# Convolution steps and bank copies re-ordered at the block boundaries of a decoder layer's up projection, and one weight sum moved from a DMA to VectorE

## The chip, the core and the metric

The kernel runs on one core of a Trainium2 chip. The metric is the device time of one execution in microseconds (us). TensorE does the matmuls, ScalarE (ACT in the profile) and VectorE (DVE) the elementwise work, GpSimd (POOL) and SyncE (SP) mostly issue DMAs.

## What is computed

The reference is one layer of a decoder for 512 prompt tokens and 8 sample tokens (520 columns), width 2048, in float32. The part that the change touches is the ConvFFN:

```python
h = rmsnorm(x, lw['ffn_norm_w']) @ lw['w_up']              # 2048 -> 2 * 5632
hp = jnp.concatenate([conv_buf, h], axis=1)
hc = cw[0] * hp[:, 0:L] + cw[1] * hp[:, 1:L + 1] + cw[2] * hp[:, 2:L + 2] + lw['conv_b']
hg, hu = jnp.split(hc, 2, axis=-1)
x = x + (jax.nn.silu(hg) * hu) @ lw['w_down']
```

Around it stand an input projection with attention and a gated spatial mix before, and a per-layer embedding gate after.

## The kernel before

**Layout and matmuls.** Activations lie transposed: 128 features on the partitions, 520 tokens in two halves of 260 columns. Every float32 matmul is made of three, since each operand is split into a part `hi` that is rounded to float32r and a rest `lo`: hi·hi, hi·lo, lo·hi.

**The weight stream.** All weights come as blocks of eight 128x128 tiles (512 KB, 128x1024 elements) in one fixed order. At the start of block v (`block_start`, L252) the program issues the loads that the table `acts` names for this block, and splits block v+2: ScalarE casts it to `hi` (L249), VectorE subtracts for `lo` (L250). There are three buffers each for `hi` and `lo`, so the cast for v+2 waits until TensorE is through with block v-1. In effect each engine gets its work for a boundary when TensorE passes that boundary, and TensorE has two more blocks before it needs the result.

**The up projection** (`ffn_up`, L1275; `wpair`, L341) works on 44 pairs: gate tile j and up tile 44+j together. Each pair is done by a Winograd-like 2x2 scheme with seven products in place of eight. A product is one block: 8 weight tiles, 3 matmuls each, 24 matmuls of 260 columns (L381). The products run in the order P5, P1, P2, P6, P4, P7, P3 and gather in four PSUM banks: P5 and P3 in bank b, P1, P6 and P7 in bank a, P2 in c, P4 in d. Between two products in one bank, ScalarE copies the bank to SBUF (`snap`, L351: `sn` after P5 and P1, `un` after P6 and P7); the next product in that bank must wait for this copy. So P6 must not begin before `sn` has been copied from bank a after P1, one block (P2) later. VectorE forms the two results `c1` (gate) and `c2` (up) from banks and copies (L355, L360, L362, L366).

**The sums of weights.** The seven products need weight sums. `winograd` (L108) puts into `acts` a load of r21 into a buffer S and three DMAs that add to S in place (r22, r11, r12), a load of r11 into a buffer L and one DMA that adds r21 to it, and plain loads of r12 and r22 (buffers `st`). The adding DMAs are issued by GpSimd (L261). S + r11 is needed by the cast for P6, S + r12 by the cast for P3, L + r21 by the cast for P7.

**The convolution.** `conv_half` (L1244) and `conv_pair` (L1261) are generators. For `c2` after P7 and for `c1` after P3: VectorE multiplies by the norm's factor R into `hb` (L1250, L1251), ScalarE makes the last tap (L1252) and two small state copies (L1253, L1254), VectorE the other two taps (L1256, L1258), then ScalarE the Silu (L1265), VectorE the product with the other half (L1268, L1271), and SyncE stores it to `fd` (L1273). One `next` is made per boundary, so that VectorE's step and the ScalarE step that reads it stand at the same boundary. Within a boundary the order is: loads, cast and rest of block v+2, GpSimd's sums, convolution steps, and last the bank copies and combinations (`late`).

**The end of the stage.** In the last pair, `f_parts` (L1306) already loads back the first eleven `fd` tiles and splits them (L430 is its VectorE part). After it `flush` (L269) runs what is left of the convolution at once, and the down projection begins.

Of the kernel before, what the change touches and what calls it, by code (L numbers as in the profile page):

```python
# [171 lines left out]
class Kernel:  # L172
    def __init__(self, ctx, tc, a):
# [63 lines left out]
    def load_block(self, b):  # L237
        self.nc.sync.dma_start(self.wtmp("st", b), self.a["w"][b])

    def split_block(self, v, part=(0, BLK)):  # L240
        if v >= NV:
            return
        t = self.st[WS.src[v]]
# [4 lines left out]
        hi, lo = self.hi[v], self.lo[v]  # L248
        self.nc.scalar.copy(hi[:, c], t[:, c])  # L249
        self.nc.vector.tensor_sub(lo[:, c], t[:, c], hi[:, c].bitcast(F32))  # L250

    def block_start(self, v):  # L252
        if v > 0:
            acts = WS.acts[v]
            for what, kind, r, src in acts:
                if what == "load":
                    self.nc.sync.dma_start(self.wtmp(kind, r), self.a["w"][src])
            self.split_block(v + 2)
            for what, kind, r, src in acts:
                if what == "sum":  # L260
                    self.nc.gpsimd.dma_start(self.st[kind, r], self.a["w"][src], accum_op=ALU.add)  # L261
        for g in list(self.conv):
            if next(g, None) is None:
                self.conv.remove(g)
        for f in self.late.pop(v, ()):
            f()
        self.tick()

    def flush(self):  # L269
        for f in self.late.pop(self.pos // BLK, ()):  # L270
            f()
        for g in self.conv:
            for _ in g:
                pass
        self.conv = []

    def at_block(self, ahead, f):
        self.late[self.pos // BLK + ahead].append(f)

    def tick(self):  # L280
        for g in list(self.bg):
# [56 lines left out]
            if k == nk - 1:  # L338
                done(n, ps[n])

    def wpair(self, name, n1, n2, X, done1, done2):  # L341


        nc = self.nc
        bank, c = {}, {}
        part = lambda t, h: t[:, h * HW:(h + 1) * HW]

        def snap(z, key, h):
            if key not in c:
# [1 line left out]
            nc.scalar.copy(part(c[key], h), bank[z][:, 0:HW])  # L351

        def after_p2():
            c["c1"] = self.slot(name="c1")
            nc.vector.tensor_add(part(c["c1"], 0), bank["c"][:, 0:HW], part(c["sn"], 0))  # L355

        def after_p7():
            c["c2"] = self.slot(name="c2")
            snap("a", "un", 1)
            nc.vector.scalar_tensor_tensor(out=part(c["c2"], 1), in0=bank["a"][:, 0:HW], scalar=-1.0, in1=part(c["sn"], 1),  # L360
                                           op0=ALU.mult, op1=ALU.subtract)
            nc.vector.tensor_sub(part(c["c2"], 0), bank["d"][:, 0:HW], part(c["un"], 1))  # L362
            done2(c["c2"])

        def after_p3():
            nc.vector.tensor_add(part(c["c1"], 1), bank["b"][:, 0:HW], part(c["un"], 0))  # L366
            done1(c["c1"])

        after = {"P5": lambda: snap("b", "sn", 1), "P1": lambda: snap("a", "sn", 0), "P2": after_p2, "P6": lambda: snap("a", "un", 0),
                 "P7": after_p7, "P3": after_p3}  # L370
        for p in PRODUCTS:
            z = BANK[p]
            new = z not in bank
            if new:
                bank[z] = self.aux("w" + z)
            ps = bank[z][:, 0:HW]
            for i in range(len(X[p])):
                whi, wlo = self.wtile((name, p, n1, i))
                xh, xl = X[p][i][:, 0:HW], X[p][i][:, HW:NT]
                for q, (w, x) in enumerate(((whi, xh), (whi, xl), (wlo, xh))):  # L380
                    nc.tensor.matmul(ps, lhsT=w, rhs=x, start=new and i == 0 and q == 0, stop=i == len(X[p]) - 1 and q == 2,  # L381
                                     skip_group_check=True)
# [853 lines left out]
    def conv_input(self, n):

        hb = self.slot(name="hb")
        self.nc.gpsimd.memset(hb[:, 0:2], 0.0)
        sv = hb[:, 2 + S:2 + S + 3 * NS].rearrange("p (b r) -> p b r", b=NS)  # L1240
        self.nc.gpsimd.tensor_copy(sv[:, :, 0:2], self.sc[:, n, :].rearrange("p (b r) -> p b r", b=NS))
        return hb

    def conv_half(self, hb, t, n):  # L1244
# [3 lines left out]
        sv = hb[:, 2 + S:2 + S + 3 * NS].rearrange("p (b r) -> p b r", b=NS)
        R, tv = self.v2(self.R), self.v2(t)
        nc.vector.tensor_mul(hb[:, 2:2 + S].rearrange("p (h w) -> p h w", h=2), tv[:, :, 0:HP], R[:, :, 0:HP])  # L1250
        nc.vector.tensor_mul(sv[:, :, 2].rearrange("p (h w) -> p h w", h=2), tv[:, :, HP:HW], R[:, :, HP:HW])  # L1251
        nc.scalar.activation(t[:, 0:m], hb[:, 2:2 + m], AF.Identity, scale=self.col("cw2", n), bias=self.col("cb", n))  # L1252
        nc.scalar.copy(self.cst[:, n, 0:2], hb[:, S:S + 2])  # L1253
        nc.scalar.copy(self.cst[:, n, 2:2 + NS], sv[:, :, 2])  # L1254
        yield True
        nc.vector.scalar_tensor_tensor(out=t[:, 0:m], in0=hb[:, 1:1 + m], scalar=self.col("cw1", n), in1=t[:, 0:m],  # L1256
                                       op0=ALU.mult, op1=ALU.add)
        nc.vector.scalar_tensor_tensor(out=t[:, 0:m], in0=hb[:, 0:m], scalar=self.col("cw0", n), in1=t[:, 0:m],  # L1258
                                       op0=ALU.mult, op1=ALU.add)

    def conv_pair(self, j, hg, tg, tu):  # L1261
        nc = self.nc
        m = S + 3 * NS
        yield from self.conv_half(hg, tg, j)
        nc.scalar.activation(tg[:, 0:m], tg[:, 0:m], AF.Silu)  # L1265
        yield True
        fv = self.v2(hg)
        nc.vector.tensor_mul(fv[:, :, 0:HP], tg[:, 0:S].rearrange("p (h w) -> p h w", h=2),  # L1268
                             tu[:, 0:S].rearrange("p (h w) -> p h w", h=2))
        sm = lambda z: z[:, S + 2:S + 2 + 3 * NS].rearrange("p (h w r) -> p h w r", h=2, r=3)[:, :, :, 0]  # L1270
        nc.vector.tensor_mul(fv[:, :, HP:HW], sm(tg), sm(tu))  # L1271
        yield True
        nc.sync.dma_start(self.fd[j], hg[:, 0:NT])  # L1273

    def ffn_up(self):  # L1275
        nc, a = self.nc, self.a
# [6 lines left out]
        def begin(g):  # L1283
            self.drain(self.gr)
            next(g)
            self.conv.append(g)

        for j in range(KF):
            if j == KF - 1:
                self.finish_fine()  # L1290
# [1 line left out]
            hg, hu = self.conv_input(j), self.conv_input(KF + j)
            up = []

            def done2(t, j=j, hu=hu, up=up):
                up.append(t)
                begin(self.conv_half(hu, t, KF + j))

            def done1(t, j=j, hg=hg, up=up):
                begin(self.conv_pair(j, hg, t, up[0]))  # L1300

            self.wpair("up", j, KF + j, self.X, done1, done2)
# [232 lines left out]
```

## Time and profile before

| | us |
|---|---|
| runs of the kernel: 3090.12, 3087.09, 3089.05; median | 3089.05 |
| the profiled execution's own time | 3091.61 |
| its span, first to last instruction | 3089.9 |
| up projection, from its first matmul (L381) to the end of its last, in the span | 1157.4 to 2368.8 |
| TensorE busy, whole span | 2836.5 |
| mean granted TensorE clock | 0.947 |

The profile is of one execution. A group's row gives the line, engine, operation and operands, the count, the busy time and the mean of one, then the engine's idle time just before these instructions and what ended it. A row of stretches gives busy time and instruction count per engine, then the granted TensorE clock (1.00 is full), the DMA engines' busy share and GB/s. A row of the timeline gives the start, the duration, the engine and the instruction, and in brackets an idle time before it with its releaser. SPq and POOLq are DMA issues; the time to landing runs from the issue to the completion.

### The profile page before, as it was taken

To read this page: it belongs to the slowest core of one execution; us is meant where nothing else is said; L and a number is where in the kernel's file an instruction comes from. 1 tells how busy PE (TensorE), PEld (TensorE's weight loads), DVE (VectorE), ACT (ScalarE), POOL (GpSimd) and SP (SyncE) were. 2 spreads that over 40 slices of the span, in tenths; PEclk is the share of its full clock that TensorE was granted. 3 is DMA by queue.
4 is the path that set the end of the run, shared out by engine and by line. 5 is a ranking of instruction groups with operands and counts; after the bars stand their busy time and mean duration, and the time that the engine had idled before them with its cause. 6 is when DMAs were issued, how large, how long until landed. Compare 5 with 4: busy or idle time off the path is not lost.

```text
span 3089.9 us, 53347 instructions
## 1 busy us (share of the span) xinstructions
PE 2836.5 (92%) x22836; PEld 2824.4 (91%) x22836; DVE 1528.7 (49%) x2265; ACT 1093.2 (35%) x1775; POOL 219.7 (7%) x425
## 2 busy tenths in 40 slices
PE   9999999999999987888888888888888999999999
PEld 9999999999999987887777887777888999999999
DVE  5666454533334356555555555555556333324543
ACT  5465432222223344334333334334334222232321
POOL 0101000000000001111111111111110000000000
PEclk9999999999999998888888888888888999999999
DMA  5223232323323455666666676666676433332232
GB/s 172 96 76 125 69 102 89 92 83 96 96 89 121 144 156 140 164 171 162 163 161 164 167 171 165 156 165 164 168 170 183 151 125 113 117 102 90 85 125 86
DMA packets 124429, 404.08 MB, mean 131 GB/s; under 512 B 14160, under 2 KB 15312, under 8 KB 124192
## 3 DMA queue, kind: packets, MB, share of 16 engines
q1 hardware_dynamic: 97344, 303.49, 30.0%
q0 software_dynamic: 26848, 97.18, 17.0%
q8 instruction: 179, 2.93, 0.4%
q14 instruction: 58, 0.48, 0.0%
HBM read 375.49 MB, written 25.12 MB: 130 GB/s over the span
## 4 chain that ended last, share of the span: by engine, by line
PE 74%; DVE 11%; ACT 8%; issue 6%; DMA 0%; SPq 0%; ACTq 0%; POOL 0%; DVEq 0%
PE mm L318 19%; PE mm L322 19%; PE mm L320 19%; PE wa L381 11%; ACT hi L249 6%; PE wd L381 4%; DVE lo L250 4%; DVE c L1258 2%; DVE c L1256 2%; ACT sn L351 1%; DVE c L366 0%; ACT cst L1253 0%; DVE hb L1251 0%; PE po L916 0%; DVE c L362 0%
## 5 line engine op out<-in xcount | busy, mean ns | idle before, releaser
L250 DVE TENSOR_TENSOR lo<-st,hi 128x1024 fp32r<-128x1024 f32 (+1 forms) x398 | 485.3, 1220 | 723.5 <-ACT hi L249 719.4
L381 PE MATMUL wa<-X,hi 128*128 128x260 f32 x2112 | 466.4, 322 | 229.9 <-ACT sn L351 229.9
L249 ACT CAST hi<-st 128x1024 fp32r<-128x1024 f32 (+1 forms) x398 | 414.3, 1041 | 684.3 <-PE mm L320 439.1
L381 PEld LDWEIGHTS wa<-X,hi 128*128 128x128 f32 x2112 | 390.1, 226 | 239.4 <-ACT sn L351 239.4
L318 PE MATMUL mm<-xnh,hi 128*128 128x260 f32 x1920 | 394.6, 288 | 5.5 <-ACT hi L249 5.5
L320 PE MATMUL mm<-xnl,hi 128*128 128x260 f32 x1920 | 386.9, 282 | 0.3 <-DVE xnl L433 0.3
L322 PE MATMUL mm<-xnh,lo 128*128 128x260 f32 x1920 | 386.9, 283 | 0.0
L381 PE MATMUL wa<-X,lo 128*128 128x260 f32 x1056 | 331.4, 314 | 0.0
L318 PEld LDWEIGHTS mm<-xnh,hi 128*128 128x128 f32 x1920 | 296.1, 189 | 5.6 <-ACT hi L249 5.5
L320 PEld LDWEIGHTS mm<-xnl,hi 128*128 128x128 f32 x1920 | 300.1, 191 | 0.6 <-DVE xnl L433 0.6
L250 DVE TENSOR_TENSOR lo<-S,hi 128x1024 fp32r<-128x1024 f32 x132 | 161.8, 1226 | 272.7 <-ACT hi L249 272.7
L322 PEld LDWEIGHTS mm<-xnh,lo 128*128 128x128 f32 x1920 | 294.0, 189 | 0.0
L318 PE MATMUL mm<-fh,hi 128*128 128x260 f32 x1408 | 283.1, 283 | 2.8 <-DVE c L366 2.8
L322 PE MATMUL mm<-fh,lo 128*128 128x260 f32 x1408 | 283.1, 283 | 0.0
L320 PE MATMUL mm<-fl,hi 128*128 128x260 f32 x1408 | 282.7, 282 | 0.0
L381 PE MATMUL wb<-X,hi 128*128 128x260 f32 x1408 | 257.6, 285 | 8.4 <-DVE xr L1197 8.4
L381 PEld LDWEIGHTS wa<-X,lo 128*128 128x128 f32 x1056 | 238.0, 225 | 0.0
L381 PEld LDWEIGHTS wb<-X,hi 128*128 128x128 f32 x1408 | 219.0, 190 | 8.5 <-issue 8.5
L249 ACT CAST hi<-S 128x1024 fp32r<-128x1024 f32 x132 | 138.2, 1047 | 238.4 <-PE wa L381 170.3
L261 POOL DMA_DIRECT2D S<-in_w x132 | 114.4, 867 | 1486.1 <-DVE lo L250 972.7
L318 PEld LDWEIGHTS mm<-fh,hi 128*128 128x128 f32 x1408 | 216.8, 188 | 3.0 <-issue 3.0
L322 PEld LDWEIGHTS mm<-fh,lo 128*128 128x128 f32 x1408 | 216.9, 188 | 0.0
(286 smaller groups left out, 5017.4 us busy)
## 6 DMA issues: line engine op xcount, KB each, us to landing
st<-in_w SPq DMA_DIRECT2D x395, 512.0 KB, 3.6
S<-in_w POOLq DMA_DIRECT2D x132, 512.0 KB, 6.5
S<-in_w SPq DMA_DIRECT2D x44, 512.0 KB, 3.5
L<-in_w SPq DMA_DIRECT2D x44, 512.0 KB, 4.4
L<-in_w POOLq DMA_DIRECT2D x44, 512.0 KB, 6.3
fd<-hb SPq DMA_DIRECT2D x44, 260.0 KB, 2.2
fr<-fd SPq DMA_DIRECT2D x44, 260.0 KB, 4.0
x<-in_x SPq DMA_DIRECT2D x16, 260.0 KB, 6.1
```

The source lines that it names most:

```text
L249: self.nc.scalar.copy(hi[:, c], t[:, c])
L250: self.nc.vector.tensor_sub(lo[:, c], t[:, c], hi[:, c].bitcast(F32))
L261: self.nc.gpsimd.dma_start(self.st[kind, r], self.a["w"][src], accum_op=ALU.add)
L318: mm(ps[:, h, 0:HW], lhsT=whi, rhs=xh[:, h, :], start=start, stop=False)
L320: mm(ps[:, h, 0:HW], lhsT=whi, rhs=xl[:, h, :], start=False, stop=False)
L322: mm(ps[:, h, 0:HW], lhsT=wlo, rhs=xh[:, h, :], start=False, stop=stop)
L351: nc.scalar.copy(part(c[key], h), bank[z][:, 0:HW])
L381: nc.tensor.matmul(ps, lhsT=w, rhs=x, start=new and i == 0 and q == 0, stop=i == len(X[p]) - 1 and q == 2, skip_group_check=True)
L1256: nc.vector.scalar_tensor_tensor(out=t[:, 0:m], in0=hb[:, 1:1 + m], scalar=self.col("cw1", n), in1=t[:, 0:m], op0=ALU.mult, op1=ALU.add)
L1258: nc.vector.scalar_tensor_tensor(out=t[:, 0:m], in0=hb[:, 0:m], scalar=self.col("cw0", n), in1=t[:, 0:m], op0=ALU.mult, op1=ALU.add)
```

## The change

`block_start` now has a fixed order by kind: loads; bank copies ("snap"); the cast for block v+2 on ScalarE; convolution steps of ScalarE ("act"); steps of VectorE ("dve"); the rest of block v+2 on VectorE; GpSimd's sums or the sum on VectorE; and what is left ("end"). The convolution is no longer a generator: each step is put down by kind for a boundary of its own, one engine's step per boundary, so that what it reads was made at a boundary before. The sum of r11 into S is no longer a DMA from memory: VectorE adds the buffer L, which holds r11 already, to S ("vsum").

```diff
-        acts[v - 2] += [("load", "st", r22, r22), ("sum", "S", r21, r11)]
+        acts[v - 2] += [("load", "st", r22, r22), ("vsum", "S", r21, ("L", r11))]
...
     def block_start(self, v):
+        acts = WS.acts[v] if v > 0 else ()
+        for what, kind, r, src in acts:
+            if what == "load":
+                self.nc.sync.dma_start(self.wtmp(kind, r), self.a["w"][src])
+        self.run_late("snap", v)
         if v > 0:
-            acts = WS.acts[v]
-            for what, kind, r, src in acts:
-                if what == "load":
-                    self.nc.sync.dma_start(self.wtmp(kind, r), self.a["w"][src])
-            self.split_block(v + 2)
-            for what, kind, r, src in acts:
-                if what == "sum":
-                    self.nc.gpsimd.dma_start(self.st[kind, r], self.a["w"][src], accum_op=ALU.add)
-        for g in list(self.conv):
-            if next(g, None) is None:
-                self.conv.remove(g)
-        for f in self.late.pop(v, ()):
+            self.cast_block(v + 2)
+        self.run_late("act", v)
+        self.run_late("dve", v)
+        if v > 0:
+            self.rest_block(v + 2)
+        for what, kind, r, src in acts:
+            if what == "sum":
+                self.nc.gpsimd.dma_start(self.st[kind, r], self.a["w"][src], accum_op=ALU.add)
+            elif what == "vsum":
+                self.nc.vector.tensor_add(self.st[kind, r], self.st[kind, r], self.st[src])
+        self.run_late("end", v)
+        self.tick()
...
+        after = {"P5": [("snap", lambda: snap("b", "sn", 1))], "P1": [("snap", lambda: snap("a", "sn", 0))], "P2": [("dve", c11)],
+                 "P6": [("snap", lambda: snap("a", "un", 0))], "P7": [("snap", lambda: snap("a", "un", 1)), ("dve", c22)],
+                 "P3": [("dve", c12)]}
...
+        states("c2", KF + j)
+        self.at_block(0, lambda: states("c1", j))
+        self.at_block(1, lambda: rstd("c2"), "dve")
+        self.at_block(2, lambda: tap2("c2", KF + j), "act")
+        self.at_block(2, lambda: rstd("c1"), "dve")
+        self.at_block(3, lambda: tap2("c1", j), "act")
+        self.at_block(3, lambda: taps01("c2", KF + j), "dve")
+        self.at_block(4, lambda: taps01("c1", j), "dve")
+        self.at_block(5, silu, "act")
+        self.at_block(6, product, "dve")
+        self.at_block(7, lambda: nc.sync.dma_start(self.fd[j], hb["c1"][:, 0:NT]))
```

The operations in the steps (`rstd`, `tap2`, `taps01`, `silu`, `product`, the combinations `c11`, `c22`, `c12`) are those of before, with the same shapes; `c12` now also makes the half of `c2` that was made after P7. `at_block(n, ...)` counts from the boundary behind P3, which is the next pair's boundary before P5. `flush` runs the steps that are left after the last pair, boundary by boundary, with no matmul between them.

Three places on the engines show the move. First ScalarE, around P5 and P1 of one pair of the middle. Names: `hi<-st`, `hi<-S`, `hi<-L` are casts of weight blocks, `sn<-wb` and `sn<-wa` the bank copies after P5 and P1, `c<-hb,cvt` the last tap, `c<-c` the Silu. Before, from the boundary ahead of P5:

```order
L249 CAST hi_21179<-st_21037 128x1024
L1252 ACTIVATE c_1229_21044<-hb_20924,cvt 128x536
L1253 COPY cst<-hb_20924 128x2
L1254 COPY cst<-hb_20924 128x8
L249 CAST hi_21219<-S_20884 128x1024
L1265 ACTIVATE c_1229_21044<-c_1229_21044 128x536
L351 COPY sn_21227<-wb_21178 128x260
L249 CAST hi_21254<-st_21101 128x1024
L351 COPY sn_21227<-wa_21216 128x260
```

After, from the boundary behind P5, with the new line numbers (L364 bank copy, L246 cast, L1267 last tap):

```order
L364 COPY sn_21201<-wb_21162 128x260
L246 CAST hi_21203<-S_20875 128x1024
L364 COPY sn_21201<-wa_21198 128x260
L246 CAST hi_21236<-st_21091 128x1024
L1267 ACTIVATE c_1230_21131<-hb_21159,cvt 128x536
L1268 COPY cst<-hb_21159 128x2
L1269 COPY cst<-hb_21159 128x8
L246 CAST hi_21271<-L_20951 128x1024
L1267 ACTIVATE c_1227_21031<-hb_21171,cvt 128x536
```

Before, a tap, its state copies, the cast for P6 and the Silu stand ahead of the two bank copies; now each bank copy is the first thing of its boundary, and the tap stands behind the cast.

Second VectorE. Before, from the boundary ahead of P5; `c_1122` is the up half, `c_1119` the gate half of the pair gone by:

```order
L250 TENSOR_TENSOR lo_18452<-st_18309,hi_18451 128x1024
L1256 SCALAR_TENSOR_TENSOR c_1122_18411<-hb_18199,cvt,c_1122_18411 128x536
L1258 SCALAR_TENSOR_TENSOR c_1122_18411<-hb_18199,cvt,c_1122_18411 128x536
L366 TENSOR_TENSOR c_1119_18316<-wb_18202,un_18347 128x260
L1250 TENSOR_TENSOR hb_18196<-c_1119_18316,R_888_12943 128x512
L1251 TENSOR_TENSOR hb_18196<-c_1119_18316,R_888_12943 128x8
L250 TENSOR_TENSOR lo_18492<-S_18156,hi_18491 128x1024
L1256 SCALAR_TENSOR_TENSOR c_1119_18316<-hb_18196,cvt,c_1119_18316 128x536
L1258 SCALAR_TENSOR_TENSOR c_1119_18316<-hb_18196,cvt,c_1119_18316 128x536
```

After, from the boundary ahead of P7 to the one behind it (L252 is the rest, L276 the sum of r11, L1283 and L1286 the product, L372 a combination):

```order
L252 TENSOR_TENSOR lo_18366<-S_18147,hi_18365 128x1024
L276 TENSOR_TENSOR S_18147<-S_18147,L_18223 128x1024
L1283 TENSOR_TENSOR hb_18195<-c_1107_18055,c_1110_18155 128x2x256
L1286 TENSOR_TENSOR hb_18195<-c_1107_18055,c_1110_18155 128x2x4
L372 SCALAR_TENSOR_TENSOR c_1120_18403<-wa_18222,sn_18225 128x260
L252 TENSOR_TENSOR lo_18399<-L_18223,hi_18398 128x1024
```

The sum of r11 is now a VectorE instruction right behind the rest for P5, and the steps of the convolution stand ahead of the rest of their boundary instead of behind it.

Third GpSimd's queue over one pair. Before (S265 belongs to one pair and S269 to the next):

```order
L261 DMA S265_17660<-in_w 128x1024
L261 DMA L264_17745<-in_w 128x1024
L1239 MEMSET hb_1103_17948 128x2
L1241 COPY hb_1103_17948<-sct_12949 128x8x2
L1239 MEMSET hb_1104_17951 128x2
L1241 COPY hb_1104_17951<-sct_12949 128x8x2
L261 DMA S269_17908<-in_w 128x1024
L261 DMA S265_17660<-in_w 128x1024
```

After:

```order
L274 DMA L264_17727<-in_w 128x1024
L1257 MEMSET hb_1101_17935 128x2
L1258 COPY hb_1101_17935<-sct_12949 128x8x2
L274 DMA S269_17899<-in_w 128x1024
L1257 MEMSET hb_1103_17947 128x2
L1258 COPY hb_1103_17947<-sct_12949 128x8x2
L274 DMA S265_17651<-in_w 128x1024
```

The adding DMA of r11 is gone; those of r21 into L, of r22 into the next pair's S and of r12 into this pair's S follow each other.

More of the change, by code (lines that the diff above doesn't have):

```diff
@@ L193, in __init__ @@
         self.late = defaultdict(list)
-        self.conv = []
         self.slotp = {}
@@ L238, in load_block, with cast_block @@
         self.nc.sync.dma_start(self.wtmp("st", b), self.a["w"][b])
-    def split_block(self, v, part=(0, BLK)):
+    def cast_block(self, v, part=(0, BLK)):
         if v >= NV:
             return
-        t = self.st[WS.src[v]]
         if part[0] == 0:
@@ L247, in split_block @@
         c = slice(part[0] * 128, part[1] * 128)
-        hi, lo = self.hi[v], self.lo[v]
-        self.nc.scalar.copy(hi[:, c], t[:, c])
-        self.nc.vector.tensor_sub(lo[:, c], t[:, c], hi[:, c].bitcast(F32))
-    def block_start(self, v):
-        if v > 0:
-            acts = WS.acts[v]
-            for what, kind, r, src in acts:
-                if what == "load":
-                    self.nc.sync.dma_start(self.wtmp(kind, r), self.a["w"][src])
-            self.split_block(v + 2)
-            for what, kind, r, src in acts:
-                if what == "sum":
-                    self.nc.gpsimd.dma_start(self.st[kind, r], self.a["w"][src], accum_op=ALU.add)
-        for g in list(self.conv):
-            if next(g, None) is None:
-                self.conv.remove(g)
-        for f in self.late.pop(v, ()):
+        self.nc.scalar.copy(self.hi[v][:, c], self.st[WS.src[v]][:, c])
@@ new lines, in rest_block, with split_block @@
+    def rest_block(self, v, part=(0, BLK)):
+        if v >= NV:
+            return
+        c = slice(part[0] * 128, part[1] * 128)
+        self.nc.vector.tensor_sub(self.lo[v][:, c], self.st[WS.src[v]][:, c], self.hi[v][:, c].bitcast(F32))
+    def split_block(self, v, part=(0, BLK)):
+        self.cast_block(v, part)
+        self.rest_block(v, part)
+    def block_start(self, v):
+        acts = WS.acts[v] if v > 0 else ()
[3 more added lines that the diff above has]
+        self.run_late("snap", v)
+        if v > 0:
+            self.cast_block(v + 2)
[10 more added lines that the diff above has]
+        self.tick()
@@ L266, in block_start, with run_late @@
+    def run_late(self, kind, v):
+        for f in self.late.pop((kind, v), ()):
             f()
-        self.tick()
     def flush(self):
[L270 to L278, printed above, removed]
+        for v in range(self.pos // BLK, self.pos // BLK + 16):
+            for kind in ("snap", "act", "dve", "end"):
+                self.run_late(kind, v)
@@ L280, in tick, with at_block @@
+    def at_block(self, ahead, f, kind="end"):
+        self.late[kind, self.pos // BLK + ahead].append(f)
     def tick(self):
@@ L339, in ngroup, with wpair @@
                 done(n, ps[n])
-    def wpair(self, name, n1, n2, X, done1, done2):
+    def wpair(self, name, n1, n2, X):
         nc = self.nc
         bank, c = {}, {}
-        part = lambda t, h: t[:, h * HW:(h + 1) * HW]
+        part = lambda key, h: c[key][:, h * HW:(h + 1) * HW]
+        ps = lambda z: bank[z][:, 0:HW]
         def snap(z, key, h):
@@ L350, in snap, with c11, c22, c12 @@
                 c[key] = self.slot(name=key)
-            nc.scalar.copy(part(c[key], h), bank[z][:, 0:HW])
-        def after_p2():
+            nc.scalar.copy(part(key, h), ps(z))
+        def c11():
             c["c1"] = self.slot(name="c1")
-            nc.vector.tensor_add(part(c["c1"], 0), bank["c"][:, 0:HW], part(c["sn"], 0))
-        def after_p7():
+            nc.vector.tensor_add(part("c1", 0), ps("c"), part("sn", 0))
+        def c22():
             c["c2"] = self.slot(name="c2")
-            snap("a", "un", 1)
-            nc.vector.scalar_tensor_tensor(out=part(c["c2"], 1), in0=bank["a"][:, 0:HW], scalar=-1.0, in1=part(c["sn"], 1),
+            nc.vector.scalar_tensor_tensor(out=part("c2", 1), in0=ps("a"), scalar=-1.0, in1=part("sn", 1),
                                            op0=ALU.mult, op1=ALU.subtract)
[L362 to L370, printed above, removed]
+        def c12():
+            nc.vector.tensor_add(part("c1", 1), ps("b"), part("un", 0))
+            nc.vector.tensor_sub(part("c2", 0), ps("d"), part("un", 1))
+        after = {"P5": [("snap", lambda: snap("b", "sn", 1))], "P1": [("snap", lambda: snap("a", "sn", 0))], "P2": [("dve", c11)],
+                 "P6": [("snap", lambda: snap("a", "un", 0))], "P7": [("snap", lambda: snap("a", "un", 1)), ("dve", c22)],
+                 "P3": [("dve", c12)]}
         for p in PRODUCTS:
@@ L375, in wpair @@
                 bank[z] = self.aux("w" + z)
-            ps = bank[z][:, 0:HW]
             for i in range(len(X[p])):
@@ L380, in wpair @@
                 for q, (w, x) in enumerate(((whi, xh), (whi, xl), (wlo, xh))):
-                    nc.tensor.matmul(ps, lhsT=w, rhs=x, start=new and i == 0 and q == 0, stop=i == len(X[p]) - 1 and q == 2,
+                    nc.tensor.matmul(ps(z), lhsT=w, rhs=x, start=new and i == 0 and q == 0, stop=i == len(X[p]) - 1 and q == 2,
                                      skip_group_check=True)
                 next(self.fine, None)
-            if p in after:
-                self.at_block(0, after[p])
+            for kind, f in after.get(p, ()):
+                self.at_block(0, f, kind)
+        return c
     def woperands(self, xb):
@@ L1233, in w_out, with conv_pair @@
         self.bg.append(self.gr)
[L1236 to L1244, printed above, removed]
+    def conv_pair(self, j, c):
         nc = self.nc
         m = S + 3 * NS
[L1248 to L1273, printed above, removed]
+        hb = {}
@@ new lines, in conv_pair, with states, rstd @@
+        sv = lambda k: hb[k][:, 2 + S:2 + S + 3 * NS].rearrange("p (b r) -> p b r", b=NS)
+        def states(k, n):
+            hb[k] = self.slot(name="hb")
+            nc.gpsimd.memset(hb[k][:, 0:2], 0.0)
+            nc.gpsimd.tensor_copy(sv(k)[:, :, 0:2], self.sc[:, n, :].rearrange("p (b r) -> p b r", b=NS))
+        def rstd(k):
+            self.drain(self.gr)
+            R, tv = self.v2(self.R), self.v2(c[k])
+            nc.vector.tensor_mul(hb[k][:, 2:2 + S].rearrange("p (h w) -> p h w", h=2), tv[:, :, 0:HP], R[:, :, 0:HP])
+            nc.vector.tensor_mul(sv(k)[:, :, 2].rearrange("p (h w) -> p h w", h=2), tv[:, :, HP:HW], R[:, :, HP:HW])
@@ new lines, in tap2, with taps01 @@
+        def tap2(k, n):
+            nc.scalar.activation(c[k][:, 0:m], hb[k][:, 2:2 + m], AF.Identity, scale=self.col("cw2", n), bias=self.col("cb", n))
+            nc.scalar.copy(self.cst[:, n, 0:2], hb[k][:, S:S + 2])
+            nc.scalar.copy(self.cst[:, n, 2:2 + NS], sv(k)[:, :, 2])
+        def taps01(k, n):
+            t = c[k]
+            nc.vector.scalar_tensor_tensor(out=t[:, 0:m], in0=hb[k][:, 1:1 + m], scalar=self.col("cw1", n), in1=t[:, 0:m],
+                                           op0=ALU.mult, op1=ALU.add)
+            nc.vector.scalar_tensor_tensor(out=t[:, 0:m], in0=hb[k][:, 0:m], scalar=self.col("cw0", n), in1=t[:, 0:m],
+                                           op0=ALU.mult, op1=ALU.add)
@@ new lines, in silu, with product @@
+        def silu():
+            nc.scalar.activation(c["c1"][:, 0:m], c["c1"][:, 0:m], AF.Silu)
+        def product():
+            tg, tu, fv = c["c1"], c["c2"], self.v2(hb["c1"])
+            nc.vector.tensor_mul(fv[:, :, 0:HP], tg[:, 0:S].rearrange("p (h w) -> p h w", h=2),
+                                 tu[:, 0:S].rearrange("p (h w) -> p h w", h=2))
+            sm = lambda z: z[:, S + 2:S + 2 + 3 * NS].rearrange("p (h w r) -> p h w r", h=2, r=3)[:, :, :, 0]
+            nc.vector.tensor_mul(fv[:, :, HP:HW], sm(tg), sm(tu))
@@ L1281, in ffn_up @@
         self.f = {}
[L1283 to L1286, printed above, removed]
         for j in range(KF):
@@ L1291, in ffn_up @@
                 self.fine = self.f_parts(ff_chunks()[0], 4)
[L1292 to L1302, printed above, removed]
+            self.conv_pair(j, self.wpair("up", j, KF + j, self.X))
         self.flush()
```

## Prediction

> **What bounds the kernel now.** The page's line of busy times comes first, then TensorE's waits, which name for each wait who ended it: its total, how often, and the longest.
>
> ```profile
> PE 2836.5 (92%) x22836; PEld 2824.4 (91%) x22836; DVE 1528.7 (49%) x2265; ACT 1093.2 (35%) x1775; POOL 219.7 (7%) x425
> PE wa L381 <- ACT sn L351: 229.9, 44, 7.3
> ```
>
> TensorE is the bound, and nearly all its waiting is of one kind: 44 waits, one per pair, for the copy of bank a after P1. TensorE's timeline has one such wait (in brackets, 5.14), and the one behind the stage (2.80):
>
> ```profile
> 1697.56 0.80 PE L381 MATMUL wa<-X,hi 128*128 128x260 f32 x2 [5.14 <-ACT sn L351]
> ...
> 2371.61 0.48 PE L318 MATMUL mm<-fh,hi 128*128 128x260 f32 x2 [2.80 <-DVE c L366]
> ```
>
> The table of stretches then shows what such a wait costs besides itself (us; busy time and count of PE, PEld, DVE, ACT, POOL; clock; DMA share; GB/s).
>
> ```profile
> 600.00:1000.00 400.00, 400.00 (x3333) 399.84 (x3332) 148.75 (x178) 100.01 (x119) 1.64 (x3) 1.00 0.31 96
> 1500.00:1800.00 300.00, 243.45 (x1848) 241.09 (x1847) 166.34 (x231) 117.48 (x199) 42.41 (x88) 0.87 0.68 164
> 1692.20:1697.56 5.36, 0.22 (x3) 0.01 (x1) 2.99 (x4) 2.57 (x6) 0.86 (x1) 0.73 0.36 44
> 1697.56:1701.57 4.01, 4.01 (x18) 4.01 (x19) 3.20 (x5) 0.89 (x1) 0.00 (x0) 0.51 0.71 161
> 1701.57:1719.50 17.93, 17.93 (x152) 17.91 (x150) 8.93 (x13) 7.27 (x13) 2.99 (x7) 1.00 0.77 200
> 2371.60:2376.00 4.40, 4.38 (x36) 4.40 (x37) 3.61 (x7) 2.36 (x8) 0.57 (x1) 1.00 0.26 102
> ```
>
> Undisturbed, 3333 matmuls take 400 us: 0.120 us each, so a pair of 7 x 24 = 168 matmuls needs 20.16 us and one block 2.88 us. In the up projection the clock averages 0.87. One pair in slices: the wait of 5.14 us, then 18 matmuls at a granted clock of 0.51 in 4.01 us, where 18 x 0.120 = 2.16 would do (1.85 us lost), then full clock. The last row follows the wait of 2.80 us and shows 1.00: a short wait costs no clock.
>
> Why the copy is late is read from the timeline of ScalarE and VectorE over one pair; TensorE ended P2 at 1719.5.
>
> ```profile
> 1717.89 0.84 ACT L1252 ACTIVATE c<-hb,cvt 128x536 f32<-128x536 f32 x1 [3.94 <-DVE hb L1251]
> 1718.82 1.04 ACT L249 CAST hi<-S 128x1024 fp32r<-128x1024 f32 x1
> 1722.66 0.65 ACT L1265 ACTIVATE c<-c 128x536 f32<-128x536 f32 x1 [2.79 <-DVE c L1258]
> 1723.21 0.36 ACT L351 COPY sn<-wb 128x260 f32<-128x260 f32 x1
> 1723.47 1.05 ACT L249 CAST hi<-st 128x1024 fp32r<-128x1024 f32 x1
> 1724.41 0.38 ACT L351 COPY sn<-wa 128x260 f32<-128x260 f32 x1
> ...
> 1717.09 0.69 DVE L1250 TENSOR_TENSOR hb<-c,R 128x512 f32<-128x512 f32 x1
> 1719.89 1.23 DVE L250 TENSOR_TENSOR lo<-S,hi 128x1024 fp32r<-128x1024 f32 x1 [2.04 <-ACT hi L249]
> 1721.04 0.77 DVE L1256 SCALAR_TENSOR_TENSOR c<-hb,cvt,c 128x536 f32<-128x536 f32 x1
> 1721.85 0.78 DVE L1258 SCALAR_TENSOR_TENSOR c<-hb,cvt,c 128x536 f32<-128x536 f32 x1
> ```
>
> ScalarE and VectorE hand work to and fro at one boundary. The tap waits 3.94 us for VectorE; the cast stands behind the tap; VectorE's rest waits for the cast; VectorE's taps stand behind the rest; the Silu waits 2.79 us for the taps; the copies `sn` stand behind the Silu. Both engines are idle much of that time; only the order is late. ScalarE reaches the copy 4.9 us after P2 is done.
>
> **The change, part by part: the steady pairs.** Two Silu rows, the first pair's and the last but one's, give the period.
>
> ```profile
> 1202.66 0.65 ACT L1265 ACTIVATE c<-c 128x536 f32<-128x536 f32 x1 [1.49 <-DVE c L1258]
> 2351.24 0.65 ACT L1265 ACTIVATE c<-c 128x536 f32<-128x536 f32 x1 [2.79 <-DVE c L1258]
> ```
>
> 42 periods in 1148.58 us: 27.35 us each. With the bank copy first at its boundary it waits only for TensorE, and P6 finds it done a block ahead. The wait, the slow matmuls behind it (5.14 + 1.85 = 6.99) and 0.2 of small gaps go: 27.35 - 20.16 = 7.19 us a pair, 42 x 7.19 = 302.0 us.
>
> What is late next? A pair's load on VectorE now, and rows for what is added:
>
> ```profile
> 1699.23:1726.52 27.29, 22.15 (x169) 21.93 (x169) 15.12 (x23) 10.71 (x18) 3.85 (x8) 0.88 0.68 164
> L250 DVE TENSOR_TENSOR lo<-S,hi 128x1024 fp32r<-128x1024 f32 x132 | 161.8, 1226 | 272.7 <-ACT hi L249 272.7
> L430 DVE TENSOR_TENSOR fl<-fr,fh 128x520 fp32r<-128x520 f32 x11 | 7.2, 695 | 3.1 <-ACT fh L429 3.1
> ```
>
> VectorE has 15.12 us of work a pair, ScalarE 10.71. The sum on VectorE has the shape and the two SBUF operands of the rest, 1.23 us; by the 512-wide row of 0.69 it could be 1.38. So VectorE has 16.3 to 16.5 of 20.16 us, ScalarE 10.71. The fullest two boundaries (ahead of P6 and of P4) hold four taps (3.1), a combination (0.42) and two rests (2.46), 5.98 us in 5.76; the boundary behind them holds a rest and the sum, 2.46 in 2.88, and gives it back. A rest has two blocks, 5.76 us, and needs 1.05 + 1.23 of it. Cost: 0; if that cover went, the excess of a boundary, some 0.2 us a pair.
>
> **The DMAs.** GpSimd's adding DMAs drop from three plus one to two plus one per pair, but the pair shrinks as well. The sum of r12 into S is the one to watch: issued behind the rest for P6, wanted by the cast for P3. Its rows before, alone and in a burst, and the DMA engines in two stretches, loads and sums:
>
> ```profile
> 1721.42 0.86 POOL L261 DMA_DIRECT2D S<-in_w  x1 [8.59 <-DVE lo L250]
> DMA to landing us min/median/max: 5.7/5.7/5.7
> DMA to landing us min/median/max: 3.5/5.7/7.5
> 1706.00:1709.50 3.50, 3.50 (x32) 3.50 (x31) 1.54 (x2) 1.62 (x3) 0.86 (x1) 1.00 0.83 329
> 1711.00:1718.00 7.00, 7.00 (x61) 7.00 (x60) 4.66 (x9) 2.07 (x5) 1.83 (x6) 1.00 1.04 204
> ```
>
> The first landing row is of that DMA alone (5.7), the second of all DMAs into S over the pair around it (up to 7.5 behind two others). Count from the boundary ahead of P1. The cast and rest for P6 end about 2.4 later, the DMA goes out 0.3 after that (1721.12 to 1721.42), at 2.7. P3 begins five blocks on, at 14.4, and needs cast and rest, 2.3, before. So the DMA may take 14.4 - 2.3 - 2.7 = 9.4 us; the rows say 5.7 to 7.5. That looks free, but the burst is new: `fd`, three loads and all three sums now come close together. At 329 GB/s `fd` and the loads (0.266 + 3 x 0.524 MB) take 5.6 us, at 204 GB/s the sums 3 x 2.57 = 7.7: 13.3 us in one piece. It starts with `fd`, behind the product on VectorE: about 1.3 us after the boundary behind P7 if VectorE keeps up, 3.1 if it is late. With 1 us to the first bytes and 1 us at the end (estimates from the 5.7 alone against 2.57 of transfer) the last sum lands 16.6 or 18.4 us after that boundary, 10.8 or 12.6 on the count above; the limit is 12.1. So 0 or 0.5 us of waiting a pair; with sums 10% longer, 1.3. I take 0.2, since the on-time row is nearest: 42 x 0.2 = 8.4 us, bounds 0 and 1.3 x 42 = 55.
>
> The Trainium skill prices this otherwise: DMA: Bandwidth & Descriptors, section on the anatomy of a DMA by the GpSimd path, fits 2.0 us plus the bytes over 436 GB/s, an estimate of 3.2 us for one such sum. The trace's 5.7 us alone contradicts it for adding DMAs; by the page nothing would be left to wait for and the 8.4 us would be 0.
>
> **First and last pair.**
>
> ```profile
> 1157.40 0.77 PE L381 MATMUL wb<-X,hi 128*128 128x260 f32 x2 [8.35 <-DVE xr L1197]
> 1176.60 0.80 PE L381 MATMUL wa<-X,hi 128*128 128x260 f32 x2 [7.31 <-ACT sn L351]
> 1175.24 1.04 ACT L249 CAST hi<-st 128x1024 fp32r<-128x1024 f32 x1
> 1176.18 0.36 ACT L351 COPY sn<-wa 128x260 f32<-128x260 f32 x1
> 2354.48 0.80 PE L381 MATMUL wa<-X,hi 128*128 128x260 f32 x2 [6.72 <-ACT sn L351]
> ```
>
> In the first pair there is no convolution to reorder; the copy stands behind operand building. Only the cast of 1.04 (0.94 to the next start) comes out from ahead of it: -0.9. Against it, the pair's VectorE sum falls into the chain that ends in the 8.35 wait for `xr`: +1.2. Net +0.3, bounds -1 and +3. In the last pair 6.72 + 1.85 = 8.6 goes, but the 11 splits (7.2 us) bring VectorE to some 22 us in 20.16, and the flush now holds one combination and one more multiply by R; both meet in the wait of 2.80 us behind the stage. I give back 3 (0 to 6): net -5.6.
>
> **The sum.** 302.0 - 8.4 - 0.3 + 5.6 = 298.9. Against the profiled execution's 3091.61 (span 3089.9 and 1.7 around it) that is 2792.7; it lies 2.6 above the median of the runs, 3089.05, so the forecast is 2790 us.
>
> **Rivals.** (1) The DMA burst binds: with VectorE late the sum of r12 lands late in every pair, and lateness keeps VectorE late. For it: DMA share 1.04 through 7 us already. Against: a first pair with its own long wait lets the DMAs run ahead. Price: 1.3 us instead of 0.2, +46: 2836. (2) The change doesn't do what it says: the hand-over survives in a new place, the Silu waiting for taps on an overfull VectorE with the copy of P7 behind it. Half the old wait, 2.6 us a pair without loss of clock: +109, 2899. Against: 16.4 of 20.16. (3) The clock stays at the stage's 0.87 without waits: 168 x 0.120 / 0.87 = 23.2, +3.0 x 42 = 126: 2916. Against: the 1.00 over 17.93 us amid DMA share 0.77. (4) Slower: GpSimd can't make descriptors beside a VectorE that is busy 16.4 of 20.16 us instead of 15.12 of 27.29, and adding DMAs get long. Each us above 9.4 is a us a pair; the old time is reached at a wait of 7.19 - 1.85 = 5.3, a landing of 14.7. At 17 it is (7.6 + 1.85 - 7.19) x 42 = +95 on 3089: 3184. Against: the issue at 1721.42 took 0.86 us although VectorE's taps ran then. The Trainium skill (SBUF — State Buffer, section on its two sides) says that VectorE in a two-port mode locks GpSimd out from writing descriptors; no run here shows such a lock.
>
> **How the numbers follow.** Chances: forecast 0.70, (1) 0.17, (2) 0.06, (3) 0.04, (4) 0.03, a third of that near no change. About 0.2%, 6 us, is what a measurement of this kernel can tell from none. So faster 0.97, same 0.01, slower 0.02. The range takes the forecast with its bounds (no DMA wait, no loss at the ends: 2776) and rival 1 with its upper bound (2790 - 8 + 55 + 6 = 2843): 2775 to 2843 leaves out 2, 3 and 4.
>
> **What would show it.** Right: no wait of P6 for `sn`, granted clock 1.00 over the middle stage, Silu rows 20.2 to 20.4 apart, VectorE at 0.8 of the stage, GpSimd's landings under 9.4. Rival 1 shows as waits of P3 for a cast that a DMA released; 2 as waits for a copy `un` or for a rest with VectorE full; 3 as a clock under 1 without waits; 4 as landings of 15 us. The forecast is wrong if a wait of over 1 us comes in every pair.

## The result, and the profile after

The changed kernel takes 2844.37 us (median of 4 runs, 2843.43 to 2846.91), the kernel before 3088.85 in the same comparison: a ratio of 0.921 (95% interval 0.9194 to 0.9226). The profiled execution took 2843.61 us with a span of 2841.9. It is faster, as forecast, by 248.0 us on profiled executions in place of 298.9, and 1.4 us beyond the range.

TensorE's waits after the change (waited for, total, times, longest):

```profile
PE wb L391 <- DVE lo L252: 28.4, 39, 0.8
PE wb L391 <- DVE xr L1208: 9.6, 1, 9.6
PE wb L391 <- ACT hi L246: 9.3, 20, 1.0
PE wa L391 <- ACT sn L364: 7.1, 2, 6.9
```

The 44 waits for the bank copy are down to two, of which the first pair has 6.9 us. New are short waits on bank b: P3 waits for its weights, first for the cast `hi`, two matmuls later for the rest `lo`, as in this pair:

```profile
1721.00 0.51 PE L391 MATMUL wb<-X,hi 128*128 128x260 f32 x2 [0.66 <-ACT hi L246]
1722.26 0.39 PE L391 MATMUL wb<-X,lo 128*128 128x260 f32 x1 [0.75 <-DVE lo L252]
```

The listed waits for `lo` and `hi` come to 37.7 us, less than the 42 x 1.43 us that are lost (below): matmuls overlap in the timeline, and around a wait they don't, so that part of the loss is counted as busy. In this pair 1.41 us are listed, and the third matmul of P3 begins 1.8 us later than it would. A stretch in the middle, with the columns of before:

```profile
1500.00:1800.00 300.00, 288.42 (x2356) 283.44 (x2356) 223.23 (x308) 148.40 (x252) 61.38 (x98) 1.00 0.73 184
```

The clock is granted in full, VectorE is busy 0.74, ScalarE 0.49, the DMA engines 0.73. So neither the clock nor a full engine takes the missing time. The Silu rows give the periods, the first four and the one that answers to the last of before:

```profile
1206.51 0.66 ACT L1279 ACTIVATE c<-c 128x536 f32<-128x536 f32 x1
1226.59 0.65 ACT L1279 ACTIVATE c<-c 128x536 f32<-128x536 f32 x1
1247.91 0.65 ACT L1279 ACTIVATE c<-c 128x536 f32<-128x536 f32 x1
1269.58 0.65 ACT L1279 ACTIVATE c<-c 128x536 f32<-128x536 f32 x1
...
2113.29 0.65 ACT L1279 ACTIVATE c<-c 128x536 f32<-128x536 f32 x1
```

42 periods in 906.78 us are 21.59 us each, 1.43 above the floor of 20.16 where the forecast had 0.2: 42 x 1.23 = 51.7 us, which is the shortfall of 50.9 within 1 us. And the first period is 20.08 us, the floor; the next are 21.32 and 21.67. TensorE itself says the same: P3 begins at 1206.93, 1227.03 and 1247.13 in the second to fourth pair, 20.10 us apart, and only behind the last of these does it wait. The kernel starts without the loss and drifts into it.

What P3 waits for, from the chain of waits of one pair (start, duration, piece):

```profile
1701.32 1.22 DVE S L276
1702.54 0.61 DVE hb L1283
...
1703.60 1.23 DVE lo L252
...
1705.69 0.99 POOL hb L1258
1706.67 0.80 POOL S L274
...
1707.59 1.04 POOL hb L1258
...
1708.89 10.93 DMA S<-in_w
...
1719.90 1.05 ACT hi L246
```

The adding DMA of r12 into S takes 10.9 us, half the period, and the cast for P3 follows it. The same in the timeline of ScalarE, with VectorE's row behind that cast, and of SyncE and GpSimd in the pair after it:

```profile
1719.90 1.99 ACT L246 CAST hi<-S 128x1024 fp32r<-128x1024 f32 x2 [3.69 <-DMA S<-in_w]
...
1720.98 2.36 DVE L252 TENSOR_TENSOR lo<-S,hi 128x1024 fp32r<-128x1024 f32 x2 [3.21 <-ACT hi L246]
1723.38 1.22 DVE L276 TENSOR_TENSOR S<-S,L 128x1024 f32<-128x1024 f32 x1
1724.52 0.69 DVE L1283 TENSOR_TENSOR hb<-c,c 128x512 f32<-128x512 f32 x1
```

```profile
1725.48 0.33 SPq L1298 DMA_DIRECT2D fd<-hb  x1
1725.90 0.80 SPq L264 DMA_DIRECT2D L<-in_w  x1
1726.75 2.29 SPq L264 DMA_DIRECT2D st<-in_w  x2
...
1727.17 0.86 POOL L274 DMA_DIRECT2D L<-in_w  x1 [17.42 <-DVE lo L252]
1728.68 0.86 POOL L274 DMA_DIRECT2D S<-in_w  x1
1730.95 0.86 POOL L274 DMA_DIRECT2D S<-in_w  x1 [0.26 <-DVE lo L252]
```

One store, three loads and three adding DMAs go out within 5.5 us. The stretches show what the DMA engines make of it:

```profile
1726.50:1740.40 13.90, 13.90 (x118) 13.90 (x117) 10.49 (x16) 5.81 (x12) 4.38 (x7) 1.00 0.97 242
1740.40:1746.00 5.60, 4.77 (x38) 4.36 (x38) 3.51 (x4) 3.75 (x5) 0.00 (x0) 1.00 0.21 61
```

They are full for 13.9 us and then little used for 5.6 (a share of 0.21). It is rival 1 of the prediction: a loop. The cast for P3 is late; on VectorE, in order, the rest for P3, the rest for P5, the sum and the product are late behind it; the store waits for the product, the loads stand behind the store, the sum into L waits for the next rest; so the piece of DMA work starts late, and its last part is the sum for the next P3.

### The profile page after: what moved, and what is told of

It reads as the page before. It is cut to its first block, busy times and chain, and to the rows that moved or that the text cites. A ratio compares the mean times of both kernels' runs of the same rounds, so it can differ in the third digit from the quotient of the medians.

```text
span 2841.9 us, 53344 instructions
## 1 busy us (share of the span) xinstructions
PE 2771.4 (98%) x22836; PEld 2753.5 (97%) x22836; DVE 1564.8 (55%) x2309; ACT 1090.1 (38%) x1775; POOL 237.1 (8%) x381
## 4 chain that ended last, share of the span: by engine, by line
PE 66%; DMA 15%; DVE 8%; POOL 4%; issue 4%; ACT 2%; DVEq 0%; SPq 0%; ACTq 0%; POOLq 0%
PE mm L330 21%; PE mm L334 20%; PE mm L332 20%; DMA S<-in_w 15%; DVE lo L252 4%; POOL hb L1258 3%; ACT hi L246 2%; DVE S L276 2%; POOL S L274 1%; PE wa L391 1%; DVE hb L1283 1%; PE wb L391 1%; PE po L927 1%; PE s L864 1%; PE pt L909 0%
## 5 line engine op out<-in xcount | busy, mean ns | idle before, releaser
L252 DVE TENSOR_TENSOR lo<-st,hi 128x1024 fp32r<-128x1024 f32 (+1 forms) x398 | 484.8, 1219 | 591.9 <-ACT hi L246 589.9
L246 ACT CAST hi<-st 128x1024 fp32r<-128x1024 f32 (+1 forms) x398 | 415.2, 1044 | 746.7 <-PE mm L332 438.2
L391 PE MATMUL wa<-X,hi 128*128 128x260 f32 x2112 | 388.1, 285 | 7.2 <-ACT sn L364 7.1
L391 PEld LDWEIGHTS wa<-X,hi 128*128 128x128 f32 x2112 | 326.5, 190 | 7.9 <-ACT sn L364 7.5
L391 PE MATMUL wa<-X,lo 128*128 128x260 f32 x1056 | 298.6, 283 | 0.0
L391 PE MATMUL wb<-X,hi 128*128 128x260 f32 x1408 | 264.9, 289 | 19.6 <-DVE xr L1208 9.6
L252 DVE TENSOR_TENSOR lo<-S,hi 128x1024 fp32r<-128x1024 f32 x132 | 158.0, 1223 | 141.2 <-ACT hi L246 137.6
L391 PE MATMUL wb<-X,lo 128*128 128x260 f32 x704 | 204.5, 290 | 28.4 <-DVE lo L252 28.4
L332 PEld LDWEIGHTS mm<-fl,hi 128*128 128x128 f32 x1408 | 217.3, 189 | 0.0
L391 PEld LDWEIGHTS wa<-X,lo 128*128 128x128 f32 x1056 | 200.2, 190 | 0.2 <-DVE lo L252 0.2
```

The costliest lines, as they stand in the source:

```text
L246: self.nc.scalar.copy(self.hi[v][:, c], self.st[WS.src[v]][:, c])
L252: self.nc.vector.tensor_sub(self.lo[v][:, c], self.st[WS.src[v]][:, c], self.hi[v][:, c].bitcast(F32))
L332: mm(ps[:, h, 0:HW], lhsT=whi, rhs=xl[:, h, :], start=False, stop=False)
L391: nc.tensor.matmul(ps(z), lhsT=w, rhs=x, start=new and i == 0 and q == 0, stop=i == len(X[p]) - 1 and q == 2, skip_group_check=True)
```

## The experiments

Two theories besides this one (DMA) were kept open: that VectorE, with a sum more, is what is late, and that GpSimd is, whose small state copies stand between the adding DMAs.

**The order alone** (the sum of r11 an adding DMA again):

```diff
-        acts[v - 2] += [("load", "st", r22, r22), ("vsum", "S", r21, ("L", r11))]
+        acts[v - 2] += [("load", "st", r22, r22), ("sum", "S", r21, r11)]
```

> The new order with the sum of r11 left as an adding DMA by GpSimd. Theory DMA (the three adding DMAs, the loads and the store come as one piece of 13.9 us, and the last of them lands 10.9 us after its issue, so that P3 waits): a fourth adding DMA of 2.6 us lengthens that piece, P3 or P6 waits longer, the period goes from 21.6 to 22.6 to 24.2 us, 2885 to 2955 us. Rival VectorE (its row of rest for P3, rest for P5, sum, product is what is late): without the sum of 1.2 us on VectorE the period falls to about 20.4, 2795 us.

Measured: 2885.02 us (2879.04 to 2885.24), ratio 0.934 (0.9326 to 0.9354). TensorE's waits:

```profile
PE wb L391 <- DVE lo L252: 28.7, 40, 0.8
PE wb L391 <- ACT hi L246: 27.2, 31, 1.9
```

P3 waits longer, although VectorE has 1.2 us less to do in the very row that leads to the store. Since this kernel also has a DMA more, that alone doesn't put the rival VectorE out; the kernel with both sums by VectorE, below, does. The new order brings some 203 us of the gain, the sum on VectorE 41 more. Part of the 41 is not the waiting itself:

```profile
1500.00:1800.00 300.00, 280.00 (x2217) 274.71 (x2216) 194.76 (x278) 139.64 (x235) 59.89 (x108) 0.97 0.79 196
```

The granted clock is 0.97 here and 1.00 in the changed kernel. In one pair P3's two waits are 1.36 and 0.75 us, and the clock shows 0.50 from 1704 to 1706; in the pair shown above, with 0.66 and 0.75, it stays at 1.00.

**The sum alone**, in the old order (the entry `vsum` in the table, and a branch for it in the old `block_start`):

> The old order with the sum of r11 by VectorE. Both theories: TensorE still waits about 5.1 us in every pair for the copy of bank a, since the hand-over between ScalarE and VectorE is unchanged and the sum stands where VectorE is idle: 3089 us, give or take 8. If the sum by itself brought part of the gain, it is 3040 or less.

Measured: 3090.2 us (3088.72 to 3092.85), ratio 1.001 (1.0 to 1.0019). TensorE still waits for the bank copy:

```profile
PE wa L383 <- ACT sn L353: 230.0, 44, 6.8
```

By itself the sum is worth nothing: the wait for the bank copy sets the pace there as before. It pays only with the new order.

**The sum of r12 by VectorE too**, from the `st` buffer in which r12 still lies:

```diff
-        acts[v + 1].append(("sum", "S", r21, r12))
+        acts[v + 1].append(("vsum", "S", r21, ("st", r12)))
```

> The changed kernel with the sum of r12 into S by VectorE as well (r12 still lies in its st buffer). Theory DMA: no DMA stands ahead of the cast for P3, the waits of P3 go, the period is 20.2 to 20.4 us, 2785 to 2800 us. Rival VectorE: another 1.2 us on VectorE makes it later, P3 waits more, period 22 or more, 2860 us or slower. Rival GpSimd (its state copies, stretched to 1.0 and 1.4 us beside VectorE, delay the adding DMAs): the sum into L stays behind no more copies than before, so as theory DMA.

Measured: 2780.79 us (2779.75 to 2783.91), ratio 0.9009 (0.8995 to 0.9022), the lowest of all (though within the spread of the last kernel below), and a little below what was expected. The middle of the stage:

```profile
1500.00:1800.00 300.00, 300.00 (x2509) 300.00 (x2509) 256.10 (x344) 161.63 (x270) 44.85 (x90) 1.00 0.65 171
```

TensorE is never idle, with VectorE busy 0.85, more than in the changed kernel. The rival VectorE is out.

**The sum of r12 as a plain copy** (S is overwritten; the sum for P3 is left out):

```diff
-        acts[v + 1].append(("sum", "S", r21, r12))
+        acts[v + 1].append(("plain", "S", r21, r12))
...
+            elif what == "plain":
+                self.nc.gpsimd.dma_start(self.st[kind, r], self.a["w"][src])
```

> The changed kernel, but the DMA of r12 overwrites S instead of adding to it: same issue, bytes and waits, the sum for P3 is left out. Theory DMA: it moves at the rate of a load (1.6 us in place of 2.6), lands 1 us earlier or more, the waits of P3 shrink or go: 2790 to 2820 us. Rivals VectorE and GpSimd: neither engine's work changes, so 2844 us, give or take 6.

Measured: 2793.39 us (2791.24 to 2796.43), ratio 0.9049 (0.9035 to 0.9062). What waits for what and the bytes stay; the adding in one of the seven transfers of the piece is gone, and 51 us with it. The issue did not quite stay the same: GpSimd takes 0.55 us for the plain copy and 0.86 for the adding one. TensorE's waits for the rest fall from 28.4 us in 39 waits to

```profile
PE wb L393 <- DVE lo L252: 3.9, 10, 0.7
```

**The store later**, behind the loads on SyncE's queue:

```diff
-        self.at_block(7, lambda: nc.sync.dma_start(self.fd[j], hb["c1"][:, 0:NT]))
+        self.at_block(10, lambda: nc.sync.dma_start(self.fd[j], hb["c1"][:, 0:NT]))
```

> The changed kernel with the store to fd issued three boundaries later, so that on SyncE's queue it no longer stands ahead of the pair's loads into L and st. No DMA and no work of an engine is added or taken away. If the piece of DMA work is late because its loads are held behind the store, which waits for VectorE's product: the loads go out in the quiet stretch before, the three sums have the DMA engines to themselves, the last lands in under 9.4 us and P3 no longer waits, 2785 to 2805 us. If only the amount of adding counts, or GpSimd's copies: 2844 us, give or take 10.

Measured: 2804.1 us (2798.11 to 2807.86), ratio 0.9077 (0.9063 to 0.909). No DMA is cheaper, only spread: two loads now go out ahead of the store, in the stretch that was idle (SyncE's and ScalarE's timeline):

```profile
1718.30 0.38 SPq L264 DMA_DIRECT2D L<-in_w  x1
1718.73 0.42 SPq L264 DMA_DIRECT2D st<-in_w  x1
1721.12 0.33 SPq L1298 DMA_DIRECT2D fd<-hb  x1
```

```profile
1715.54 2.00 ACT L246 CAST hi<-S 128x1024 fp32r<-128x1024 f32 x2 [2.96 <-DMA S<-in_w]
```

In the pair before these loads the last sum went out at 1706.46 and the cast behind it began at 1715.54, 9.1 us later instead of 11.0. That is just inside the 9.4 of the prediction; but some pairs still wait (8.9 us in 20 waits), where none was expected.

**The state copies on ScalarE** (`nc.scalar.copy` for `nc.gpsimd.tensor_copy`):

> The changed kernel with the copies of the convolution state into hb made by ScalarE instead of GpSimd (two per pair of about 0.2 us). Rival GpSimd: its copies, 1.0 and 1.4 us beside VectorE's work, stand between the adding DMAs; without them these go out up to 2 us earlier and the period falls to about 20.4, 2795 us. Theory DMA: the last sum waits for VectorE's rest for P6 anyway (0.26 us after the copies), and the DMA engines are busy through the piece: 2835 to 2845 us.

Measured: 2849.33 us (2847.05 to 2850.27), ratio 0.9224 (0.921 to 0.9238): not faster, and 4 us above the expectation of the theory DMA. GpSimd's timeline shows why it is no faster:

```profile
1709.13 0.86 POOL L274 DMA_DIRECT2D L<-in_w  x1 [16.93 <-DVE lo L252]
1709.71 1.21 POOL L274 DMA_DIRECT2D S<-in_w  x1
1712.96 0.86 POOL L274 DMA_DIRECT2D S<-in_w  x1 [1.93 <-DVE lo L252]
```

With the copies gone the last sum waits 1.93 us for VectorE's rest instead of 0.26. The rival GpSimd is out.

**One more DMA per pair**, to the changed kernel and to the one with both sums by VectorE:

```diff
+        self.scr = self.drp.tile([128, BLK * 128], F32, name="scr")
...
+        self.at_block(0, lambda: nc.sync.dma_start(self.scr, self.a["w"][j]))
```

> The changed kernel with one more DMA per pair: SyncE copies 512 KB from one place in memory to another, into nothing that is read, at the boundary behind P3. Theory DMA: the piece gets 1.6 us longer or more, P3 waits that much longer, 44 x 1.6 = 70, about 2915 us (2890 to 2940). Rivals VectorE and GpSimd: no change, 2844 us, give or take 8.

> The kernel with both sums by VectorE and the same extra copy per pair. Theory DMA: there the DMA work has room (two adding DMAs, none ahead of P3's cast), so the copy is hidden, 2781 to 2795 us. If the copy costs here what it costs the changed kernel, it costs by itself, not by its place: 2850 us.

Measured: the changed kernel goes to 2900.3 us (2897.91 to 2901.99), +56, 1.27 us a pair; the other to 2783.25 (2781.03 to 2785.08), ratio 0.9009 (0.8994 to 0.9024) against 0.9009 without the copy. The same DMA costs where the piece of DMA work binds and next to nothing where it does not. The 56 us are again not waiting alone: the clock from 1500 to 1800 is 0.97, which makes 20.16 / 0.97 - 20.16 = 0.6 us a pair, an estimate of about half.

**The two sums exchanged**: r12 by VectorE, r11 by an adding DMA.

> The changed kernel with the two sums exchanged: r12 by VectorE, r11 by an adding DMA again. As many adding DMAs (three) and as much VectorE work as the changed kernel. If the number of adding DMAs by itself binds: 2844 us, give or take 10. If it is the place of the last one, behind two sums and the loads and ahead of P3's cast: the sum of r11 goes out two boundaries earlier, first in line, and lands in time for P6's cast, 2785 to 2805 us.

Measured: 2784.19 us (2782.71 to 2786.4), ratio 0.9014 (0.9001 to 0.9028). As many adding DMAs and as much work on VectorE as the changed kernel, and 60 us less, just below what was expected. GpSimd's timeline:

```profile
1708.65 0.86 POOL L274 DMA_DIRECT2D S<-in_w  x1 [14.60 <-DVE lo L252]
1711.89 0.86 POOL L274 DMA_DIRECT2D L<-in_w  x1 [2.37 <-DVE lo L252]
1712.59 1.21 POOL L274 DMA_DIRECT2D S<-in_w  x1
```

The sum of r11 goes out first; the last in line is the sum for the next pair's P5, whose cast begins at 1726.12, over 13 us later. The DMA engines are no less busy (0.76 from 1500 to 1800, 0.73 in the changed kernel) and TensorE is busy all the 300 us. So the number of sums is not what binds, but the place of the last one. The exchange also moves VectorE's sum out of the row ahead of the store, so that the store goes out earlier; this run alone does not tell the two apart, but the kernel with both sums by VectorE keeps its sum in that row and is as fast.

**Both sums by VectorE and the store later**:

> Both sums by VectorE and the store to fd three boundaries later. TensorE had no waits left in the middle of the stage with both sums by VectorE, so nothing is to be gained there: 2781 us, give or take 4.

Measured: 2781.43 us (2780.99 to 2784.14), ratio 0.9008 (0.8992 to 0.9023): no gain, as expected. With TensorE busy throughout the middle, only the first and the last pair are left.

## Why the prediction was wrong

**Right: what goes.** The waits for the bank copy went, and the low clock with them (0.87 before, 1.00 after), as the steady-pair step said. In the kernel with both sums by VectorE the Silu rows are 20.10 us apart: 42 x (27.35 - 20.10), some 304 us, went where 302.0 was forecast.

**Right: VectorE's load is no bound.** The sum was to cost 1.23 us by the row of the rest; it does:

```profile
L276 DVE TENSOR_TENSOR S<-S,L 128x1024 f32<-128x1024 f32 x40 | 49.0, 1225 | 1.4
```

**Right, nearly: first and last pair.** The wait before the first pair grew from 8.35 to 9.6 us (+1.25; +1.2 in the sum; the two kernels of the new order with r11 by a DMA show 8.3), and the first pair's bank copy fell only from 7.31 to 6.9. In the last pair the wait of 6.72 went, and the wait behind the stage grew from 2.80 to 3.5, where 3 us were given back for it. The lower end of the range, 2776 by its own bounds, comes to 2777; nothing hangs on it.

**Wrong: the size of the DMA term.** The step that failed is "I take 0.2, since the on-time row is nearest". It measured 1.43 us a pair, above the upper bound of 1.3 as well, and that is the whole error within 1 us. The parts of the term:

The length of the piece was nearly right: 13.3 us forecast, 13.9 measured; from the store to the cast for P3 15.3 forecast, 15.9 measured (1725.48 to 1741.37). The last sum went out 3.1 us after the boundary ahead of P1 (1708.89, with P1's first matmul at 1705.81), 2.7 forecast. The limit fits too: in the pair of the stretches above the cast begins at 1741.37, 13.5 us after P1's first matmul at 1727.86, 1.4 beyond the limit of 12.1.

The on-time case was given 1.3 us to spare (10.8 against 12.1). GpSimd's issues of that sum and ScalarE's casts behind it, in the second, third and fourth pair, show that it had almost none:

```profile
1195.64 0.86 POOL L274 DMA_DIRECT2D S<-in_w  x1 [2.45 <-DVE lo L252]
1215.74 0.86 POOL L274 DMA_DIRECT2D S<-in_w  x1 [2.47 <-DVE lo L252]
1235.84 0.87 POOL L274 DMA_DIRECT2D S<-in_w  x1 [0.26 <-DVE lo L252]
```

```profile
1203.05 2.15 ACT L246 CAST hi<-S 128x1024 fp32r<-128x1024 f32 x2 [1.29 <-DMA S<-in_w]
1224.68 2.00 ACT L246 CAST hi<-S 128x1024 fp32r<-128x1024 f32 x2 [2.82 <-DMA S<-in_w]
1246.01 1.99 ACT L246 CAST hi<-S 128x1024 fp32r<-128x1024 f32 x2 [3.37 <-DMA S<-in_w]
```

From issue to cast 7.4, then 8.9, then 10.2 us, and 10.9 in the pair shown above. The third pair's 8.9 us is the on-time case: the store at the head of its piece had gone out at 1208.64, 1.7 us after the boundary behind P7 (1.3 forecast), and its cast came 12.0 us after P1's first matmul at 1212.66. TensorE did not wait yet, but VectorE's row behind the cast was late already. The stores behind these three casts go out 1.7, 3.2 and 4.5 us after that boundary (1208.64, 1230.27 and 1251.59 against P3's first matmuls at 1206.93, 1227.03 and 1247.13): each pair's lateness is handed to the next by the store. "A first pair with its own long wait lets the DMAs run ahead" held for two pairs.

The late case was capped too low. It had the store go out 3.1 us after the boundary behind P7. In the steady state it goes out at 1725.48, 5.1 us after P7's last matmul has ended (1720.35): P3's cast comes so late that the rest for P3, the rest for P5, the sum and the product (2.36 + 1.22 + 0.86 us) all stand between it and the store. Late VectorE was priced once, as a fixed delay, though the late cast and VectorE's own row add up.

The landings of 5.7 to 7.5 us came from an issue that stood alone or behind two others; the last sum of a piece that fills the engines for 13.9 us landed after 10.9. The sentence on the Trainium skill's fit (DMA: Bandwidth & Descriptors, anatomy of a DMA by the GpSimd path: an estimate of 3.2 us) pointed the wrong way; this case's adding DMAs land after 5.7 us alone and after 10.9 here, and a plain copy in place of one of them is worth 51 us.

The remaining rivals did not come: no wait for a later bank copy to speak of, no low clock, and GpSimd's issues still take 0.86 us. Rival 4's rate, a us a pair for each us of landing above 9.4, does fit (10.9 - 9.4 = 1.5), but not its cause.

What stays open is how much of the 51 us of the plain copy is its shorter transfer, how much its shorter issue and how much the loop that these break; the runs show the sum.

## What to carry to other kernels

When a wait is removed, lay the DMAs of one period on one line, with their issue times and the engines' rate for each kind, and see which is the last of the full stretch and who waits for that one: the share over the whole stage (0.73) hides a stretch that is full for 13.9 us. Check whether the piece's start depends on its own end; here such a loop turned a cast that had 0.1 us to spare into a steady loss of 1.43 us a pair, and changing who is last in line (60 us here, with the same work) gained nearly as much as taking that DMA away (64 us). Operands that already lie in SBUF are worth adding on an engine with room before a DMA reads them again.

## What the runs showed of the hardware

GpSimd's small state copies got longer, though nothing in them changed. The groups of the middle of the stage, before and after:

```profile
L1241 POOL COPY hb<-sct 128x16 f32<-128x16 f32 x84 | 31.5, 389 | 0.0
```

```profile
L1258 POOL COPY hb<-sct 128x16 f32<-128x16 f32 x78 | 91.9, 1186 | 0.0
```

0.39 us became 1.19 in the mean. They now run beside VectorE's instructions of 1.22 us, and each ends with one:

```profile
1705.41 1.22 DVE L252 TENSOR_TENSOR lo<-st,hi 128x1024 fp32r<-128x1024 f32 x1
...
1705.69 0.99 POOL L1258 COPY hb<-sct 128x16 f32<-128x16 f32 x1
```

The Trainium skill (SBUF — State Buffer, section on its two sides) has a VectorE instruction with two SBUF operands and a GpSimd instruction that reads SBUF exclude each other for a whole instruction; the trace agrees in so far as this copy ends at 1706.68, VectorE's instruction with two SBUF operands at 1706.63, and the next pair of the two at 1708.63 and 1708.60. Taking the copies off GpSimd brought nothing here, as the run with them on ScalarE showed.
